# Transposing DMAs of u, q and k on ScalarE's queue, and in all groups of the second MLP's first quarter

## The chip, the cores and the metric

The kernel runs on one core of a Trainium2 chip. A core has a matrix engine (TensorE, PE in the profile), two engines for elementwise work that this kernel uses all the time (VectorE, DVE, and ScalarE, ACT), a third that it hardly uses (GpSimd, POOL), a sequencer without a datapath (SyncE, SP), and 16 DMA engines. Each of the five has its own queue of instructions and runs it in order; they wait for one another by semaphores. A DMA is issued by an instruction in the queue of some engine, which stands in that queue like any other. The metric is the time on the device of one execution, in microseconds (us).

## The reference

Two layers over 256 tokens of 2048 features, in float32. Layer 0 mixes tokens by a convolution module, layer 1 by differential attention; each is followed by an MLP with squared ReLU, and each sub-layer has a scale, a shift and a gate made from a condition vector `c`:

```
mod = silu(c) @ ada_w[i] + ada_b[i]            # six vectors of 2048 per layer
h = x * (1 + scale) + shift
x = LayerNorm(alpha * x + gate * f(h))
f = conv module | differential attention       # layer 0 | layer 1
f = square(relu(h @ w1 + b1)) @ w2 + b2        # MLP: 2048 -> 8192 -> 2048
attention: q, k, v = split(h @ w_qkv); rope on q and k; 16 heads of 128 in 8 pairs;
           a = softmax(q1 k1) - lam * softmax(q2 k2); o = rmsnorm(a v) @ w_o
```

## The kernel before

The 256 tokens are two tiles, t = 0 and 1, of 128 partitions. A matmul takes the activations with features on the partitions as its stationary operand (called `h`, `u` or `attno` in their turned form) and weights 512 columns wide as its moving one, so an output has tokens on the partitions and has to be turned before it can feed the next product. To keep float32's accuracy each operand is held as a high and a low part, and a product is three matmuls: high by high (L702), high by low part of the weight (L704), low by high (L705).

**The weights.** They arrive by DMA from SP, 1 MB at a time (L638), which is two tiles of 128 rows and 512 columns for each of two halves. Each half is cast by ACT to its high part (L657, `wh_...`), VectorE subtracts for the low part (L659, `wl_...`), and PE then runs 12 matmuls on it. A group (512 output columns, all 2048 inputs) is 8 such halves. Loads and casts run four halves ahead of PE (`AHEAD = 4`). Rows of the condition matrices that are needed later come between them as loads of 1 MB too (L421), and VectorE makes dot products of them (L230).

**MLP 1** has four quarters q of its 8192 hidden features. A quarter is four groups g of w1 (512 hidden features each) and then four groups of w2. When a w1 group ends, its output for t = 0 and t = 1 has to be biased, squared, turned and split into `u_hi` (ACT, L515) and `u_lo` (VectorE, L518). There are two ways. By PE: ACT copies the output (L1483, `us`), PE transposes four blocks of 128 (L1488, `ut`), VectorE adds, rectifies and squares (L1501, L1504). By DMA: ACT copies the float32 bits into two planes of 16-bit halves (L1417, `uh`), a transposing DMA turns them (L1419, `ux`, 128 x 8 x 128), ACT puts the halves together again (L1423, `r`), and VectorE works on that (L1431, L1432). `by_dma(i, q, g)` chooses. Work that follows later is put off by `defer(n, fn)`, n halves of weights: 2 halves for PE's way (`U_WAIT`), 4 for the DMA's in layer 1 (`T_WAIT`).

**Attention** has groups of q, k and v in turn, four heads of each at a time (g = 0 to 3). `rope_evac` rotates q and k on VectorE (L1657 to L1665), ACT splits the result into two planes (L1669), a transposing DMA turns them (L1674, `qkx_q`, `qkx_k`), and four halves later ACT joins them (L1680, `qT`, `kT`). Only k's last group is turned by PE (L1686, L1689). The softmaxes (`at_sm`, L1719), the norms (`at_on`, L1750, L1753) and the turned outputs (`attno_hi`, L515; `attno_lo`, L518) of the group before lie between these on ACT and VectorE.

The order of PE's and VectorE's instructions follows the program and its deferrals. The order on ACT and SP is set by a scheduler that builds a timeline of the whole kernel; an instruction that comes to ACT therefore also changes what it puts where around it.

Of the kernel before, what the change touches and what calls it, by code (L numbers as in the profile page):

```python
# [82 lines left out]
def group_order(s):  # L83

    return list(range(NGRP))[::1 if (len(SLICES) - s) % 2 else -1]
# [72 lines left out]
def trunk(  # L158
# [8 lines left out]
    nc = tc.nc  # L167
# [16 lines left out]
    def tp_tile(name):  # L184
        return ps_tp[0].tile([P, 512], F32, tag="tp", name=name)
# [57 lines left out]
    def defer(n, fn):  # L243
        put_off.append((ticks[0] + n, fn))
# [265 lines left out]
    def put_split(pair, c0, n, s0, ns, src, eng=None, trail=False):  # L510

        hi, lo = pair
        h = hi[:, c0:c0 + n, s0:s0 + ns]
        l = lo[:, c0:c0 + n, s0:s0 + ns]
        nc.scalar.copy(h, src)  # L515

        def low():
            (eng or nc.vector).tensor_tensor(l, src, h.bitcast(F32), op=ALU.subtract)  # L518
        if trail:
            trailing.append(low)  # L520
        else:
            low()
# [739 lines left out]
    for s, (f0, nf) in enumerate(SLICES):  # L1262
# [6 lines left out]
        for pos, k in units:  # L1269
            g = group_order(s)[pos]  # L1270
# [3 lines left out]
            if (s, h) in X_AT:  # L1274
                a, b = X_AT[s, h]
# [8 lines left out]
            if nf > 1 or pos % 2 == 0:  # L1284
                parts = w_parts.pop(0)
# [14 lines left out]
            if not last and h >= END_AT[s]:  # L1300
                n = h - END_AT[s] - 1 + (s + 1 < BOTH_PE)
# [106 lines left out]
        defer(4 + q, lambda q=q: alpha_x(q))  # L1408

    def by_dma(i, q, g):  # L1410
        return i == 1 and (q > 0 or g == 3)

    def halves_t(t, ps, uT, i, q, g, n0):

        name = f"{i}_{q}_{g}_{t}"
        parts = work.tile([P, 2, NG], U16, tag="X", name=f"uh_{name}", bufs=3)
        nc.scalar.copy(parts, ps.bitcast(U16).rearrange("p (n b) -> p b n", b=2))  # L1417
        turned = work.tile([P, 2, 4, P], U16, tag="A", name=f"ux_{name}")
        nc.sync.dma_start_transpose(turned.rearrange("p b a n -> p (b a) n"), parts.rearrange("p b n -> p (b n)"))  # L1419

        def rest():
            r = work.tile([P, 4, P], F32, tag="B", name=f"r_{name}")
            nc.scalar.copy(r.rearrange("p a n -> p (a n)").bitcast(U16).rearrange("p (a n b) -> p a n b", a=4, b=2),  # L1423
                           turned.rearrange("p b a n -> p a n b"))
            f0 = i * 64 + n0 // P
            if i == 0:
                for j in range(4):
                    nc.scalar.activation(r[:, j, :], r[:, j, :], AF.Relu, bias=cv["b1c"][:, f0 + j:f0 + j + 1])
                nc.vector.tensor_tensor(r, r, r, op=ALU.mult)
            else:  # L1430
                nc.vector.tensor_tensor(r, r, cv["b1c"][:, f0:f0 + 4].unsqueeze(2).broadcast_to([P, 4, P]), op=ALU.add)  # L1431
                nc.vector.scalar_tensor_tensor(r, r, 0.0, r, ALU.max, ALU.mult)  # L1432
            put_split(uT, g * 4, 4, t * P, P, r, trail=True)
        defer(T_WAIT[i], rest)
# [218 lines left out]
    def rope_evac(nm, g, kv):  # L1653
        def on_t(t, ps):
            ph = ps.rearrange("p (h d) -> p h d", h=4)
            p1 = work.tile([P, 4, P], F32, tag="A", name=f"rp1_{nm}{g}{t}")
            nc.vector.tensor_tensor(p1.rearrange("p h (b d) -> p (h b) d", b=2),  # L1657
                                    ps.rearrange("p (h d) -> p h d", d=64),
                                    at["cos"][:, t, :].unsqueeze(1).broadcast_to([P, 8, 64]), op=ALU.mult)
            p2 = work.tile([P, 4, P], F32, tag="B", name=f"rp2_{nm}{g}{t}")  # L1660
            nc.vector.tensor_tensor(p2[:, :, 0:64], ph[:, :, 64:128],
                                    at["sinN"][:, t, :].unsqueeze(1).broadcast_to([P, 4, 64]), op=ALU.mult)
            nc.vector.tensor_tensor(p2[:, :, 64:128], ph[:, :, 0:64],
                                    at["sinP"][:, t, :].unsqueeze(1).broadcast_to([P, 4, 64]), op=ALU.mult)
            nc.vector.tensor_tensor(p1, p1, p2, op=ALU.add)  # L1665

            if (nm, g) != ("k", 3):
                parts = p2.rearrange("p h n -> p (h n)").bitcast(U16).rearrange("p (b n) -> p b n", b=2)
                nc.scalar.copy(parts, p1.rearrange("p h n -> p (h n)").bitcast(U16).rearrange("p (n b) -> p b n", b=2))  # L1669
                if t == 0:  # L1670
                    turned = late["pool"].tile([P, 2, 4, P], U16, tag="qkx", name=f"qkx_{nm}{g}{t}")
                else:
                    turned = work.tile([P, 2, 4, P], U16, tag="A", name=f"qkx_{nm}{g}{t}")
                nc.sync.dma_start_transpose(turned.rearrange("p b a n -> p (b a) n"),  # L1674
                                            parts.rearrange("p b n -> p (b n)"))

            def joined():
                if t == 0:
                    kv[nm] = work.tile([P, 4, S], F32, tag="X", name=f"{nm}T_{g}", bufs=3)
                nc.scalar.copy(kv[nm].bitcast(U16).rearrange("p h (n b) -> p h n b", b=2)[:, :, t * P:(t + 1) * P, :],  # L1680
                               turned.rearrange("p b h n -> p h n b"))

            def rest():
                pt = tp_tile(f"qkt_{nm}{g}{t}")
                for h in range(4):
                    nc.tensor.transpose(out=pt[:, h * P:(h + 1) * P], in_=p1[:, h, :], identity=ident)  # L1686
                if t == 0:
                    kv[nm] = work.tile([P, 4, S], F32, tag="X", name=f"{nm}T_{g}", bufs=3)
                nc.scalar.copy(kv[nm][:, :, t * P:(t + 1) * P], pt.rearrange("p (h n) -> p h n", h=4))  # L1689
            if (nm, g) != ("k", 3):  # L1690
                defer(4, joined)
            else:
                defer(3, rest)
        return on_t
# [233 lines left out]
```

## Time and profile before

| | us |
|---|---|
| median of 3 runs | 2267.64 (2267.3 to 2270.41) |
| the profiled execution | 2264.22 |
| its span, first to last instruction | 2262.3 |
| PE busy | 2223.8 (98%) |
| VectorE busy | 1713.5 (76%) |
| ScalarE busy | 1139.8 (50%) |

The granted clock of TensorE is 0.996 over the span. All DMAs of the kernel are issued by SP: loads of 1 MB for weights and condition rows, and 40 transposing ones of 256 KB: 8 for q, 6 for k and 26 for the `u` of MLP 1. In the rows of the profile an engine's name with q behind it (SPq, ACTq) is its queue, where issuing is shown; `x2` stands for two instructions drawn together; what stands in brackets is the idle time of the engine before an instruction and whose end finished it. PE's rows overlap, since matmuls are pipelined.

### The profile page before, as it was taken

What the parts mean: (1) busy time and instruction counts of PE and PEld (TensorE: products, weight loads), DVE (VectorE), ACT (ScalarE), POOL (GpSimd) and SP (SyncE); (2) the same over time, 40 slices, a digit from 0 to 9 for tenths busy, and PEclk for the clock granted to TensorE, in tenths of its full rate; (3) what the DMA queues carried; (4) which work ended last, traced back from release to release, by engine and by line L of the source; (5) the groups of instructions that cost most, each with busy time, mean ns of one, the idle gap of its engine ahead of it and who ended that gap; (6) DMA issues with size and microseconds to landing.
All of it is one profiled execution on the core that took longest, in us unless ns stands there. A gap on an engine that the chain in (4) does not pass through costs nothing.

```text
span 2262.3 us, 28005 instructions
## 1 busy us (share of the span) xinstructions
PE 2223.8 (98%) x10900; PEld 1779.6 (79%) x10900; DVE 1713.5 (76%) x2124; ACT 1139.8 (50%) x1528; POOL 38.2 (2%) x53
## 2 busy tenths in 40 slices
PE   8999999999999999999999999999999999999999
PEld 5677657687888888888878788787888888888886
DVE  7688889778977888878878877887965665665567
ACT  4336773564355355355365555545444643643652
POOL 0000000000000000000000010100000000000000
PEclk9999999999999999999999999999999999999999
DMA  9996789699988888888858876875976765766773
GB/s 397 419 392 270 298 323 397 218 340 330 349 301 315 308 290 319 320 306 287 292 168 280 270 228 213 288 272 178 331 247 199 209 211 191 224 202 192 220 239 111
DMA packets 259712, 619.04 MB, mean 274 GB/s; under 512 B 52623, under 2 KB 52851, under 8 KB 230011
## 3 DMA queue, kind: packets, MB, share of 16 engines
q1 hardware_dynamic: 259580, 617.27, 77.9%
q8 instruction: 85, 1.39, 0.3%
q14 instruction: 47, 0.38, 0.0%
HBM read 604.59 MB, written 2.15 MB: 268 GB/s over the span
## 4 chain that ended last, share of the span: by engine, by line
PE 85%; DVE 7%; DMA 3%; ACT 3%; issue 1%; POOL 0%; SPq 0%; ACTq 0%; DVEq 0%; POOLq 0%
PE w_ps L704 20%; PE w_ps L705 20%; PE w_ps L702 19%; PE pw_ps L600 2%; PE pw_ps L601 2%; PE pw_ps L602 2%; PE cv L936 1%; PE pw_ps L702 1%; PE pw_ps L705 1%; PE pw_ps L704 1%; PE qkv_q_ps L705 1%; PE qkv_q_ps L702 1%; PE qkv_v_ps L704 1%; PE qkv_q_ps L704 1%; PE qkv_v_ps L705 1%
## 5 line engine op out<-in xcount | busy, mean ns | idle before, releaser
L657 ACT CAST wh_w<-w_w 128x1024 fp32r<-128x1024 f32 x512 | 535.9, 1053 | 658.1 <-PE w_ps L705 507.9
L659 DVE TENSOR_TENSOR wl_w<-w_w,wh_w 128x1024 fp32r<-128x1024 f32 x510 | 613.6, 1222 | 314.5 <-ACT wh_w L657 314.1
L702 PE MATMUL w_ps<-wh_w,hm_hi 128*128 128x512 f32 x1024 | 401.0, 392 | 2.5 <-ACT hm_hi L515 2.5
L705 PE MATMUL w_ps<-wh_w,hm_lo 128*128 128x512 f32 x1024 | 399.6, 390 | 1.6 <-DVE hm_lo L518 1.6
L704 PE MATMUL w_ps<-wl_w,u_hi 128*128 128x512 f32 x1024 | 399.1, 390 | 1.6 <-DVE wl_w L659 1.6
L702 PE MATMUL w_ps<-wh_w,u_hi 128*128 128x512 f32 x1024 | 399.1, 390 | 0.0
L704 PE MATMUL w_ps<-wl_w,hm_hi 128*128 128x512 f32 x1024 | 399.0, 390 | 0.0
L705 PE MATMUL w_ps<-wh_w,u_lo 128*128 128x512 f32 x1024 | 398.5, 389 | 0.0
L230 DVE SCALAR_TENSOR_TENSOR adaw<-adaw,cond_rows 128x2048 f32<-128x2048 f32 x108 | 246.8, 2285 | 0.2 <-DMA adaw<-in_ada_rows_dram 0.2
L702 PEld LDWEIGHTS w_ps<-wh_w,hm_hi 128*128 128x128 f32 x1024 | 192.7, 188 | 44.1 <-ACT hm_hi L515 4.1
L704 PEld LDWEIGHTS w_ps<-wl_w,u_hi 128*128 128x128 f32 x1024 | 192.3, 188 | 43.4 <-DVE wl_w L659 3.8
L705 PEld LDWEIGHTS w_ps<-wh_w,hm_lo 128*128 128x128 f32 x1024 | 192.6, 188 | 42.9 <-DVE hm_lo L518 2.9
L702 PEld LDWEIGHTS w_ps<-wh_w,u_hi 128*128 128x128 f32 x1024 | 192.3, 188 | 40.2
L704 PEld LDWEIGHTS w_ps<-wl_w,hm_hi 128*128 128x128 f32 x1024 | 192.6, 188 | 39.5
L705 PEld LDWEIGHTS w_ps<-wh_w,u_lo 128*128 128x128 f32 x1024 | 192.3, 188 | 39.8
L600 PE MATMUL pw_ps<-wh_pw,h_hi 128*128 128x512 f32 x256 | 103.9, 406 | 2.6 <-ACT wh_pw L582 1.9
L601 PE MATMUL pw_ps<-wl_pw,h_hi 128*128 128x512 f32 x256 | 100.8, 394 | 0.9 <-DVE wl_pw L585 0.8
L602 PE MATMUL pw_ps<-wh_pw,h_lo 128*128 128x512 f32 x256 | 100.5, 393 | 0.0
L585 DVE TENSOR_TENSOR wl_pw<-w_pw,wh_pw 128x1024 fp32r<-128x1024 f32 x64 | 77.3, 1221 | 28.9 <-ACT wh_pw L582 28.7
L582 ACT CAST wh_pw<-w_pw 128x1024 fp32r<-128x1024 f32 x64 | 65.9, 1051 | 44.8 <-PE pw_ps L602 25.3
L600 PEld LDWEIGHTS pw_ps<-wh_pw,h_hi 128*128 128x128 f32 x256 | 48.4, 189 | 29.6 <-issue 13.0
L518 DVE TENSOR_TENSOR u_lo<-r,u_hi 128x512 fp32r<-128x512 f32 x64 | 43.5, 689 | 28.4 <-ACT u_hi L515 28.2
(355 smaller groups left out, 3012.1 us busy)
## 6 DMA issues: line engine op xcount, KB each, us to landing
w_w<-in_mlp_w_dram SPq DMA_DIRECT2D x256, 1024.0 KB, 5.9
adaw<-in_ada_rows_dram SPq DMA_DIRECT2D x108, 1024.0 KB, 6.7
w_pw<-in_pw_tiles_dram SPq DMA_DIRECT2D x32, 1024.0 KB, 12.4
ad<-in_ada_rows_dram SPq DMA_DIRECT2D x25, 1024.0 KB, 8.5
w_pw<-in_conv_pw_w_dram SPq DMA_DIRECT2D x16, 1024.0 KB, 9.1
w_qkv_q<-in_attn_qkv_w_dram SPq DMA_DIRECT2D x16, 1024.0 KB, 5.4
w_qkv_k<-in_attn_qkv_w_dram SPq DMA_DIRECT2D x16, 1024.0 KB, 5.1
w_qkv_v<-in_attn_qkv_w_dram SPq DMA_DIRECT2D x16, 1024.0 KB, 7.1
```

Of the source, the lines that this page charges most:

```text
L230: nc.vector.scalar_tensor_tensor(w, w, 1.0, cond_rows, ALU.mult, ALU.mult, accum_out=m[:, ch:ch + 1])
L518: (eng or nc.vector).tensor_tensor(l, src, h.bitcast(F32), op=ALU.subtract)
L582: nc.scalar.copy(hq, rq)
L585: nc.vector.tensor_tensor(lq, rq, hq.bitcast(F32), op=ALU.subtract)
L600: nc.tensor.matmul(pss[t], lhsT=xh, rhs=wh, start=(kc == first), stop=False)
L601: nc.tensor.matmul(pss[t], lhsT=xh, rhs=wl, start=False, stop=False)
L602: nc.tensor.matmul(pss[t], lhsT=xl, rhs=wh, start=False, stop=(kc == last))
L657: nc.scalar.copy(hi, rq)
L659: eng.tensor_tensor(lo, rq, hi.bitcast(F32), op=ALU.subtract)
L702: nc.tensor.matmul(pss[tt], lhsT=xh, rhs=wh, start=(kc == 0 and job["bias"] is None), stop=False)
L704: nc.tensor.matmul(pss[tt], lhsT=xh, rhs=wl, start=False, stop=False)
L705: nc.tensor.matmul(pss[tt], lhsT=xl, rhs=wh, start=False, stop=(kc == nk - 1))
```

## The change

All transposing DMAs are issued on ScalarE's queue, where SP issued them before. And `by_dma` now says yes for every group of layer 1, so that groups 0 to 2 of quarter 0 are turned by DMA as well.

```diff
     def by_dma(i, q, g):
-        return i == 1 and (q > 0 or g == 3)
+        return i == 1
...
         parts = work.tile([P, 2, NG], U16, tag="X", name=f"uh_{name}", bufs=3)
         nc.scalar.copy(parts, ps.bitcast(U16).rearrange("p (n b) -> p b n", b=2))
         turned = work.tile([P, 2, 4, P], U16, tag="A", name=f"ux_{name}")
-        nc.sync.dma_start_transpose(turned.rearrange("p b a n -> p (b a) n"), parts.rearrange("p b n -> p (b n)"))
+        nc.scalar.dma_start_transpose(turned.rearrange("p b a n -> p (b a) n"), parts.rearrange("p b n -> p (b n)"))
...
                     turned = work.tile([P, 2, 4, P], U16, tag="A", name=f"qkx_{nm}{g}{t}")
-                nc.sync.dma_start_transpose(turned.rearrange("p b a n -> p (b a) n"),
-                                            parts.rearrange("p b n -> p (b n)"))
+                nc.scalar.dma_start_transpose(turned.rearrange("p b a n -> p (b a) n"),
+                                              parts.rearrange("p b n -> p (b n)"))
```

So 46 transposing DMAs stand in ACT's queue (40 moved, 6 new); 24 PE transposes and 6 copies `us` are gone, and 6 copies `uh` and 6 copies `r` have come. SP's other instructions keep their order. Three places show how the instructions now stand.

On ACT at q's group 1 (the two copies L1669 of t = 0 and t = 1, the joined copies `qT`, casts of k's weights, and work of the attention of group 0), before:

```order
L1669 COPY rp_q_10093<-rp_q_10091 128x1024
L657 CAST wh_qkv_k_2_0_10150<-w_qkv_k_2_10148 128x1024
L1669 COPY rp_q_10102<-rp_q_10100 128x1024
L1680 COPY qT_10207<-qkx_q_10098 128x4x256
L657 CAST wh_qkv_k_2_1_10180<-w_qkv_k_2_10148 128x1024
L1680 COPY qT_10207<-qkx_q_10107 128x4x256
L1719 ACTIVATE at_1_1_sm,at_1_1_zs<-at_1_1_sm,at_1_1_mx 128x256 x2
L1750 ACTIVATE at_1_0_on,at_1_0_ss<-at_1_0_o 128x256
L657 CAST wh_qkv_k_3_0_10214<-w_qkv_k_3_10212 128x1024
L515 CAST attno_hi<-at_0_1_o_10167 128x2x128
```

and now:

```order
L1669 COPY rp_q_10093<-rp_q_10091 128x1024
L657 CAST wh_qkv_k_2_0_10150<-w_qkv_k_2_10148 128x1024
L1674 DMA_TRANSPOSE qkx_q_10098<-rp_q_10093 128x8x128
L1669 COPY rp_q_10102<-rp_q_10100 128x1024
L1680 COPY qT_10207<-qkx_q_10098 128x4x256
L1674 DMA_TRANSPOSE qkx_q_10107<-rp_q_10102 128x8x128
L657 CAST wh_qkv_k_2_1_10180<-w_qkv_k_2_10148 128x1024
L1719 ACTIVATE at_1_1_sm,at_1_1_zs<-at_1_1_sm,at_1_1_mx 128x256 x2
L1750 ACTIVATE at_1_0_on,at_1_0_ss<-at_1_0_o 128x256
L657 CAST wh_qkv_k_3_0_10214<-w_qkv_k_3_10212 128x1024
L1680 COPY qT_10207<-qkx_q_10107 128x4x256
L515 CAST attno_hi<-at_0_1_o_10167 128x2x128
```

The second transfer now stands behind the copy that waits for the first to land, and the second joined copy has moved down to just ahead of `attno_hi`.

On ACT behind the first w1 group of quarter 1 of MLP 1, before:

```order
L1417 COPY uh_1_0_0_14055<-w_1_1_0_ps_13917 128x1024
L1417 COPY uh_1_0_1_14059<-w_1_1_0_ps_13918 128x1024
L657 CAST wh_w_1_1_1_1_1_14065<-w_w_1_1_1_1_14037 128x1024
L657 CAST wh_w_1_1_1_2_0_14083<-w_w_1_1_1_2_14081 128x1024
L1423 COPY r_1_0_0_14115<-ux_1_0_0_14057 128x1024
L1423 COPY r_1_0_1_14120<-ux_1_0_1_14061 128x1024
L657 CAST wh_w_1_1_1_2_1_14099<-w_w_1_1_1_2_14081 128x1024
```

and now:

```order
L1417 COPY uh_1_0_0_14043<-w_1_1_0_ps_13905 128x1024
L1417 COPY uh_1_0_1_14047<-w_1_1_0_ps_13906 128x1024
L657 CAST wh_w_1_1_1_1_1_14053<-w_w_1_1_1_1_14025 128x1024
L1419 DMA_TRANSPOSE ux_1_0_0_14045<-uh_1_0_0_14043 128x8x128
L1419 DMA_TRANSPOSE ux_1_0_1_14049<-uh_1_0_1_14047 128x8x128
L657 CAST wh_w_1_1_1_2_0_14071<-w_w_1_1_1_2_14069 128x1024
L1423 COPY r_1_0_0_14103<-ux_1_0_0_14045 128x1024
L1423 COPY r_1_0_1_14108<-ux_1_0_1_14049 128x1024
L657 CAST wh_w_1_1_1_2_1_14087<-w_w_1_1_1_2_14069 128x1024
```

Both transfers stand together between two casts, with one cast between them and the copies `uh` that they read.

On VectorE behind group 1 of quarter 0, which was turned by PE (L230 and L842 are work of the condition vectors and of the norm), before:

```order
L230 SCALAR_TENSOR_TENSOR adaw_5_11_12940,mod_5_11778<-adaw_5_11_12940,cond_rows 128x2048
L1501 TENSOR_TENSOR r_0_1_0_12962<-ut_0_1_0_12957,vec_101 128x512
L1504 SCALAR_TENSOR_TENSOR r_0_1_0_12962<-r_0_1_0_12962 128x512
L1501 TENSOR_TENSOR r_0_1_1_12971<-ut_0_1_1_12966,vec_101 128x512
L1504 SCALAR_TENSOR_TENSOR r_0_1_1_12971<-r_0_1_1_12971 128x512
L518 TENSOR_TENSOR u_0_lo<-r_0_1_0_12962,u_0_hi 128x4x128
L518 TENSOR_TENSOR u_0_lo<-r_0_1_1_12971,u_0_hi 128x4x128
L659 TENSOR_TENSOR wl_w_1_0_2_2_0_12980<-w_w_1_0_2_2_12977,wh_w_1_0_2_2_0_12979 128x1024
L659 TENSOR_TENSOR wl_w_1_0_2_2_1_12996<-w_w_1_0_2_2_12977,wh_w_1_0_2_2_1_12995 128x1024
L230 SCALAR_TENSOR_TENSOR adaw_5_12_12999,mod_5_11778<-adaw_5_12_12999,cond_rows 128x2048
```

and now:

```order
L230 SCALAR_TENSOR_TENSOR adaw_5_11_12940,mod_5_11778<-adaw_5_11_12940,cond_rows 128x2048
L659 TENSOR_TENSOR wl_w_1_0_2_2_0_12960<-w_w_1_0_2_2_12957,wh_w_1_0_2_2_0_12959 128x1024
L659 TENSOR_TENSOR wl_w_1_0_2_2_1_12976<-w_w_1_0_2_2_12957,wh_w_1_0_2_2_1_12975 128x1024
L230 SCALAR_TENSOR_TENSOR adaw_5_12_12979,mod_5_11778<-adaw_5_12_12979,cond_rows 128x2048
L1431 TENSOR_TENSOR r_0_1_0_12994<-r_0_1_0_12994,vec_101 128x512
L1432 SCALAR_TENSOR_TENSOR r_0_1_0_12994<-r_0_1_0_12994 128x512
L1431 TENSOR_TENSOR r_0_1_1_12999<-r_0_1_1_12999,vec_101 128x512
L1432 SCALAR_TENSOR_TENSOR r_0_1_1_12999<-r_0_1_1_12999 128x512
L842 TENSOR_TENSOR z<-z,basem_gb_12955 128x512
L518 TENSOR_TENSOR u_0_lo<-r_0_1_0_12994,u_0_hi 128x4x128
L518 TENSOR_TENSOR u_0_lo<-r_0_1_1_12999,u_0_hi 128x4x128
```

The four operations on `r` come two low parts and one dot product later than before; their number and size are the same.

## The prediction

> **What bounds the kernel now.** I read the page first, to see which engine sets the span, then PE's waits, because only these can be shortened, and then the timelines at the places that the change touches.
>
> ```profile
> span 2262.3 us, 28005 instructions
> PE 2223.8 (98%) x10900; PEld 1779.6 (79%) x10900; DVE 1713.5 (76%) x2124; ACT 1139.8 (50%) x1528; POOL 38.2 (2%) x53
> PE 85%; DVE 7%; DMA 3%; ACT 3%; issue 1%; POOL 0%; SPq 0%; ACTq 0%; DVEq 0%; POOLq 0%
> ```
>
> PE is busy for 98% of the span and makes 85% of the chain of waits. SP's issuing has 0% of that chain. So a shorter queue on SP is worth nothing by itself; the change can gain only where PE has less to do or waits less, and loses where a wait that is now hidden reaches PE. These are PE's waits that lie behind a transposing DMA or just after one, and the one on the last group of MLP 1:
>
> ```profile
> PE qkt_k L1686 <- DVE rp_k L1665: 1.6, 2, 1.3
> PE w_ps L704 <- DVE wl_w L659: 1.6, 4, 0.6
> PE wo_ps L704 <- DVE wl_wo L659: 1.2, 1, 1.2
> PE qkv_k_ps L704 <- DVE wl_qkv_k L659: 1.1, 1, 1.1
> PE qkv_v_ps L704 <- DVE wl_qkv_v L659: 0.9, 1, 0.9
> ```
>
> The columns are the total in us, how many, and the longest. They sum to 6.4 us, 0.28% of the span. No measured difference under 0.2%, about 4.5 us, can be told from no change for this kernel; so the whole gain in sight is near that bound.
>
> **The transposes taken from PE.** Three w1 groups of quarter 0 give up eight PE transposes each.
>
> ```profile
> 1575.97 0.87 PE ut L1488 x8
> ...
> 1621.28 0.87 PE ut L1488 x8
> ```
>
> These are the first and the last of three alike in the chain of waits: 3 x 0.87 = -2.6 us. That is the certain part of PE's work, but it is time only where the engines that feed PE can run faster too. The windows that hold these groups say otherwise (columns: window, length, busy us and count of PE, PEld, DVE, ACT, POOL, granted clock, DMA share, GB/s):
>
> ```profile
> 1575.60:1598.30 22.70, 22.70 (x106) 18.90 (x105) 19.83 (x21) 10.53 (x12) 0.00 (x0) 1.00 0.83 281
> 1598.30:1620.90 22.60, 22.60 (x106) 18.80 (x105) 22.14 (x25) 10.44 (x12) 0.00 (x0) 1.00 0.96 340
> 1620.90:1643.50 22.60, 22.60 (x105) 18.84 (x104) 19.43 (x24) 11.28 (x12) 0.00 (x0) 1.00 0.96 353
> ```
>
> In the same stretch, 1598 to 1645, ACT's waits for loads (total, how many, longest):
>
> ```profile
> ACT wh_w L657 <- DMA w_w<-in_mlp_w_dram: 10.6, 4, 3.3
> ```
>
> A group without its transposes would last 22.6 - 0.87 = 21.7 us. The middle window has 22.14 us of VectorE work, and in the last two the DMA engines are busy for 0.96 x 22.6 = 21.7 us. ACT already waits four times for a load, 10.6 us in all. Into this stretch the change puts two more transposing DMAs per group. What one costs is in the rows of the tile that receives them:
>
> ```profile
> L1419 SPq DMA_TRANSPOSE ux<-uh x26: 1238/1276/4808, 1641.6 to 2166.5; - x26
> DMA to landing us min/median/max: 3.1/3.3/4.1
> ```
>
> Issue takes 1.28 us at the median and landing 3.3 us from the issue's start, so the engines move data for at most 3.3 - 1.28 = 2.0 us per transfer; the lower bound is zero, for a transfer that fits into gaps. In the two windows with a share of 0.96 there are no gaps to speak of, so the loads behind get late by up to 2 x 2 x 2.0 = 8 us; in the first, 0.17 x 22.7 = 3.9 us are free, which is just the 4.0 us that its two need. What takes up lateness is the lead of the weights' low parts over PE:
>
> ```profile
> 1610.17 1.22 DVE L659 TENSOR_TENSOR wl_w<-w_w,wh_w 128x1024 fp32r<-128x1024 f32 x1
> 1613.18 0.39 PE L704 MATMUL w_ps<-wl_w,hm_hi 128*128 128x512 f32 x1
> ```
>
> The part is done at 1611.39 and used at 1613.18: 1.8 us of lead. Half of the upper bound, 4 us, less one lead of 1.8 us is 2.2 us; and the 0.87 us that VectorE refuses in the middle window (22.14 against 21.7) is 0.4 more. I take +3 us, bounds 0 and 8 us: the stretch gives its own gain back.
>
> **The queue of ACT in attention.** Eight of q's transfers and six of k's now stand in ACT's order. Around q's group 1 the trace has:
>
> ```profile
> 1248.99 3.55 SPq L1674 DMA_TRANSPOSE qkx_q<-rp_q  x2
> 1252.59 0.75 SPq L638 DMA_DIRECT2D w_qkv_k<-in_attn_qkv_w_dram  x1
> 1253.77 1.17 ACT L1680 COPY qT<-qkx_q 128x1024 uint16<-128x1024 uint16 x1 [2.49 <-DMA qkx_q<-rp_q]
> 1255.79 1.16 ACT L1680 COPY qT<-qkx_q 128x1024 uint16<-128x1024 uint16 x1
> 1259.32 0.40 ACT L515 CAST attno_hi<-at_o 128x256 fp32r<-128x256 f32 x1
> 1260.70 1.22 DVE L659 TENSOR_TENSOR wl_qkv_k<-w_qkv_k,wh_qkv_k 128x1024 fp32r<-128x1024 f32 x1
> 1266.65 0.50 PE L704 MATMUL qkv_k_ps<-wl_qkv_k,ha_hi 128*128 128x512 f32 x1 [1.11 <-DVE wl_qkv_k L659]
> ```
>
> SP's two issues, 3.55 us with the wait for the second copy, end before it sends the next weight load at 1252.59. In the new order of ACT the first transfer is issued inside the 2.49 us that ACT now idles, so it costs nothing. The second stands behind the joined copy that waits for the first to land: its issue of 1.24 us falls on busy ACT, the second joined copy drops behind two exponentials, a norm and a cast, and the cast attno_hi behind that. Without new idle time attno_hi starts one issue later, 1260.6 for 1259.32. VectorE's attno_lo and the low weight part follow on its queue, and PE, which already waits 1.11 us there, waits 1.2 to 1.3 more. Queued behind are the remaining casts of k's weights, for which VectorE and then PE wait: +1.3 us.
>
> The same pieces in the same order stand at q's group 3. There VectorE idles for attno_hi as well, and the chain ends at the two waits on rope's last group, 1.6 us together:
>
> ```profile
> 1400.18 1.17 ACT L1680 COPY qT<-qkx_q 128x1024 uint16<-128x1024 uint16 x1 [0.74 <-DMA qkx_q<-rp_q]
> 1402.86 0.51 ACT L1719 ACTIVATE at_sm<-at_sm,at_mx 128x256 f32<-128x256 f32 x1 [0.56 <-DVE at_mx L1716]
> 1404.71 1.05 ACT L657 CAST wh_qkv_k<-w_qkv_k 128x1024 fp32r<-128x1024 f32 x1 [0.75 <-DMA w_qkv_k<-in_attn_qkv_w_dram]
> 1407.52 0.43 DVE L518 TENSOR_TENSOR attno_lo<-at_o,attno_hi 128x256 fp32r<-128x256 f32 x1 [2.00 <-ACT attno_hi L515]
> ```
>
> ACT's idle time in the three rows is 0.74 + 0.56 + 0.75 = 2.05 us, so of two issues, 2.5 us, some 0.5 us is left: +0.5 us. The other groups of q and k have no PE wait of their own in the list above, apart from v's 0.9 us; there I count 0. Together +2 us. Upper bound: three of the listed waits, in k, v and rope, deepened by a full issue each, 3 x 1.28 = +3.8 us. Lower bound: these three vanish because SP, without its 3.55 us, sends its load earlier, -(1.1 + 0.9 + 1.6) = -3.6 us. I stay on the positive side because each wait ends on VectorE behind ACT and none on a load.
>
> **The queue of ACT in the 13 groups of MLP 1 that turn by DMA already.** One group, from its copies to PE's first use of what follows:
>
> ```profile
> 1749.62 1.93 ACT L1417 COPY uh<-w_ps 128x1024 uint16<-128x1024 uint16 x2 [0.99 <-PE w_ps L705]
> 1750.66 2.62 SPq L1419 DMA_TRANSPOSE ux<-uh  x2
> 1751.43 1.06 ACT L657 CAST wh_w<-w_w 128x1024 fp32r<-128x1024 f32 x1
> 1753.02 1.05 ACT L657 CAST wh_w<-w_w 128x1024 fp32r<-128x1024 f32 x1 [0.53 <-PE w_ps L705]
> 1753.98 2.32 ACT L1423 COPY r<-ux 128x1024 uint16<-128x1024 uint16 x2
> 1763.39 1.22 DVE L659 TENSOR_TENSOR wl_w<-w_w,wh_w 128x1024 fp32r<-128x1024 f32 x1
> 1766.65 0.39 PE L704 MATMUL w_ps<-wl_w,hm_hi 128*128 128x512 f32 x1
> ```
>
> After the change both issues stand between the two casts. If ACT's sequencer issues them while its datapath is still in the first cast, they run from 1751.5 to 1754.05, the second cast starts there in place of 1753.02, and the two r copies end at 1757.4 in place of 1756.30: 1.1 us late. If the issue begins only when the cast is over, it is 2.1 us. The lead at the end of the chain is 1766.65 - (1763.39 + 1.22) = 2.04 us. So a group costs 0 by the first reading and 0.1 by the second: 0 to 1.3 us for 13 groups, and I take 0. This is the term with the thinnest cover: everything over 2.04 us goes to PE thirteen times.
>
> In the three groups of quarter 0 the same work is new to ACT. Of the copy that it replaces the trace has this row:
>
> ```profile
> L1483 ACT COPY us<-w_ps x6: 587/587/587, 1572.6 to 1618.6; 128x512 f32<-128x512 f32 x6
> ```
>
> For each transfer that is 2.32 / 2 = 1.16 us of r, 1.28 of issue and 1.93 / 2 - 0.59 = 0.38 of uh, 5.6 us a group, on an engine that the windows show busy for 10 to 11 of 22 us; without that room it would cost those 5.6 us. I count 0.
>
> In the last group of quarter 3 the transfers stand behind the final layer norm's two loads:
>
> ```profile
> 2164.42 6.88 SPq L1419 DMA_TRANSPOSE ux<-uh  x2
> 2164.42 9.43 DMA ux<-uh
> ```
>
> ACT's queue frees them of that, 9.43 us against some 4.6 for two issues and a landing, but of PE's four waits on low parts of the MLPs, 1.6 us in the first fence of waits, none is over 0.6: I take -0.2 us.
>
> **The sum.** -2.6 + 3.0 + 2.0 + 0 - 0.2 = +2.2 us. The profiled execution took 2264.22 us around its span of 2262.3, so it would take 2266.4; the median of the runs is 2267.64, 3.4 us above the profiled one, and the forecast in those terms is 2269.9, so 2270 us, or +0.1%: no change that can be measured. By the terms' bounds together (not all at one end) it lies between 2265 and 2275.
>
> **The rivals.** *First, slower: the transfers are stretched by the loads.* Today transfers and weight loads leave SP one after the other: the load at 1753.78 follows the second transfer's issue.
>
> ```profile
> 1753.78 5.12 SPq L638 DMA_DIRECT2D w_w<-in_mlp_w_dram  x2
> ```
>
> From ACT the second would be issued from 1752.8 to 1754.05, so its 2.0 us of data run beside that load. Were the DMA engines to alternate between two queues, it would land up to 2.2 us later, at 1758.3; the first r copy no longer hides that, and the second starts 2.0 us after its new slot of 1756.3. Its end is then 3.1 us later than now against 2.04 of lead: +1.0 us per group, 13 groups of MLP 1 and 3 of quarter 0 at 0.3 more: 13 + 4, less what the sum already counts in quarter 0, some +12 us, 2282. It decides as soon as the landing of the second transfer exceeds its present 3.3 us by about 1.1. Against it: the longest landing of all 26 today is 4.1, with loads all around. The trace of before has only one queue for all this, so it can't refuse it. The Trainium skill speaks for it: "DMA: Bandwidth & Descriptors", section "Queues, rings and completion order", says that each DMA engine takes turns between the queues that have work, a packet at a time, and its section "Issuing engines are not separate DMA queues" that issuing from several engines saves only the time of the sequencer. By that rule this rival holds; no run here shows it yet.
>
> *Second, faster: SP's block was the cost.* With the loads of attention leaving up to 3.55 us earlier and nothing late on ACT, the five waits listed first shrink to nothing and the transposes' 2.6 us are kept: at most -6.4 - 2.6 = -9, and by half of the waits 2267.6 - 5.8 = 2262. For it speaks the 3.55 us in which SP stands; against it, that SP has 0% of the chain.
>
> *Third, slower: ACT's issues don't overlap and block.* One SP issue took 4.81 us (the largest of the 26). Were an issue on ACT to wait like that in most groups, ACT would be 2.1 + 2 = 4 us late against 2.04: +2 us x 13 = 26, 2296. The median of 1.28 speaks against it.
>
> *Fourth: the moves do nothing, only quarter 0 counts*: -2.6 kept, 2265. That is inside the forecast's range.
>
> **How the numbers follow.** The forecast, with the fourth rival inside it, has 0.47; the first rival 0.30, the second 0.17, the third 0.06. Faster by over 0.2% is the second rival, 0.17. Slower takes the first and third and a little of the forecast's upper edge (2272.2 to 2275): 0.38. The rest, 0.45, is within 0.2%. The likeliest case's own range is 2265 to 2275; to leave out no more than 2 in 10, the range takes the first rival up to 2283 and the faster one down to 2262.
>
> **What would show it right or wrong.** Right: 24 fewer PE transposes, the three windows of quarter 0 no shorter than 22.3 us, the wait of k's low part at 2.3 to 2.5 us, no PE wait in quarters 1 to 3, transfers landing in 3.3 us. Wrong towards slower: a PE wait of about 1 us on u_hi, u_lo or wl_w once in each group of quarters 1 to 3, with landings over 4.4 us. Wrong towards faster: windows of 21.7 us in quarter 0, and attention's waits gone. If PE's sum of waits agrees but the time doesn't, a term I do not have is at work.

## The result: 1.3% slower, and where the time came from

The changed kernel takes 2298.94 us, median of four runs (2294.25 to 2302.49), where the kernel before takes 2268.59 beside it: a ratio of 1.0132, with a 95% interval from 1.0111 to 1.0153. That is 30 us; the forecast was 2270 with a range that ended at 2283.

From the page of the changed kernel, its span, the engines' busy times and its DMA queues (packets, MB, share of 16 engines):

```profile
span 2292.4 us, 27954 instructions
PE 2233.1 (97%) x10876; PEld 1781.5 (78%) x10876; DVE 1713.2 (75%) x2124; ACT 1148.1 (50%) x1534; POOL 40.1 (2%) x53
q1 hardware_dynamic: 217340, 606.78, 74.7%
q10 hardware_dynamic: 48576, 12.06, 3.5%
```

PE does the same matmuls less 24 transposes, and VectorE and ScalarE work as long as before. What is new is a second queue, q10: ScalarE's transfers no longer stand in line with SP's loads in q1. PE's waits of the changed kernel:

```profile
PE w_ps L702 <- ACT wh_w L657: 10.0, 3, 4.8
PE w_ps L704 <- DVE wl_w L659: 9.7, 8, 3.1
PE qkv_k_ps L704 <- DVE wl_qkv_k L659: 5.3, 2, 2.7
```

Before, these were none, 1.6 and 1.1. To see where the time arises I took, in both profiles, the moment at which PE first uses the low part of each of the 672 half tiles of weights; the growth of the difference between two halves is the delay that arises between them. Here it is for the changed kernel and every experiment below, each against the profiled execution of the kernel before (us; attention is its q, k and v groups from their fourth half on, since no transfer is issued ahead of that; quarter 0 runs from the start of its second group to the end of its fourth; the last group is what follows quarter 3's w1 groups). The expectations below have 18.8 for quarter 0, counted behind the first of PE's gains of 0.9 us, and 3.1 for the last group, an earlier reckoning.

| kernel | attention | quarter 0 | rest of MLP 1 | last group |
|---|---|---|---|---|
| changed | 6.7 | 17.9 | 0.0 | 3.6 |
| ScalarE's queue, old groups (e1) | 11.5 | 0.0 | 0.1 | 5.6 |
| SP's queue, all groups (e2) | -0.2 | 7.4 | 0.0 | -0.2 |
| q and k alone on ScalarE's queue (e3) | 8.2 | 0.5 | 0.0 | 0.7 |
| changed, rows in 2 KB pieces (e4) | 14.6 | 12.0 | 6.0 | 8.7 |
| 22 late u transfers on ScalarE's queue (e5) | 0.3 | 0.0 | 0.0 | 0.5 |
| the same, with extra loads (e6) | -0.2 | 0.0 | 30.6 | 0.4 |
| SP's queue, with extra loads (e7) | 0.1 | 0.0 | 0.0 | 0.3 |
| changed, thin rows (e8) | 7.9 | 5.8 | 0.4 | 2.8 |
| e3 with both transfers first (e9) | 8.7 | 0.0 | 0.0 | 0.5 |
| SP's queue, all groups, thin rows (e10) | -0.3 | 4.5 | 0.0 | 0.8 |
| six new transfers alone on ScalarE's queue (e11) | 0.6 | 18.6 | 0.3 | 0.3 |
| 24 late u transfers, final loads later (e12) | -0.3 | 0.0 | 0.0 | -0.5 |

The three places of the changed kernel give 28.2 of the 30.1 us by which its span is longer. The rest arises ahead of the attention and in its first halves, where the program is the same; there, around wo and ahead of quarter 0 other rows have up to 4.3 us as well, from one execution to the next.

The windows of quarter 0 in the changed kernel (length, busy us of PE, PEld, DVE, ACT, POOL with counts, granted clock, DMA share, GB/s):

```profile
1583.90:1605.80 21.90, 21.32 (x94) 17.32 (x93) 19.79 (x20) 12.65 (x15) 0.00 (x0) 1.00 0.90 288
1605.80:1631.60 25.80, 18.32 (x73) 14.42 (x73) 16.35 (x18) 10.02 (x11) 0.00 (x0) 0.83 0.92 258
1631.60:1661.00 29.40, 22.07 (x92) 17.50 (x92) 20.18 (x24) 13.13 (x14) 0.00 (x0) 0.91 1.05 272
```

The group that now begins at 1605.8 shows why. Its timeline, both transfers and who waits for them:

```profile
1604.83 1.35 ACTq L1419 DMA_TRANSPOSE ux<-uh  x1
1606.22 5.57 ACTq L1419 DMA_TRANSPOSE ux<-uh  x1
1607.95 2.59 SPq L638 DMA_DIRECT2D w_w<-in_mlp_w_dram  x2
1611.91 2.00 ACT L657 CAST wh_w<-w_w 128x1024 fp32r<-128x1024 f32 x2 [5.25 <-issue]
1616.05 1.17 ACT L1423 COPY r<-ux 128x1024 uint16<-128x1024 uint16 x1 [2.14 <-DMA ux<-uh]
1622.93 1.16 ACT L1423 COPY r<-ux 128x1024 uint16<-128x1024 uint16 x1 [5.71 <-DMA ux<-uh]
1625.09 0.80 PE L702 MATMUL w_ps<-wh_w,hm_hi 128*128 128x512 f32 x1 [4.34 <-ACT wh_w L657]
1629.02 0.79 PE L704 MATMUL w_ps<-wl_w,hm_hi 128*128 128x512 f32 x1 [3.13 <-DVE wl_w L659]
```

Two things happen to ScalarE, one after the other. It can't finish issuing the second transfer for 5.57 us, and the casts of the weights behind it stand. Then it waits twice for a transfer to land, the second time until 1622.93, 16.7 us after that transfer's issue began; the next cast stands behind that copy, and PE runs dry. The rows of the tile over all its transfers say the same (longest issue 8.57 us, longest landing 13.3 among those that the view could pair):

```profile
L1419 ACTq DMA_TRANSPOSE ux<-uh x32: 1248/1348/8568, 1582.2 to 2192.1; - x32
DMA to landing us min/median/max: 3.0/3.4/13.3
```

Why a transfer takes so long is in the packets. Counted from the trace, packets that began in each microsecond on the 16 engines together, in this group:

```
us from the start     1609  1610  1611  1612  1613  1614  1615  1616  1617  1618  1619
SP, 2 KB                 0     0    18    33    56    77   106   127   160   137   126
SP, 8 KB (rows)         46    29     1     0     0     0     0     0     0     3     3
ScalarE, 256 bytes      36   281   619   113    96    73   107   129   203   187   141
```

From 1614 on the two queues advance by about one packet each in turn, whatever the packets' sizes (73 to 77, 107 to 106, 129 to 127). In the last group of MLP 1 it is the same beside packets of 8 KB: from 2196 to 2200 ScalarE's queue begins 59, 53, 81, 86 and 136 packets in a microsecond, SP's 48, 48, 70, 83 and 133. A transposing DMA has 1024 packets of 256 bytes, 64 per engine, so beside a queue of loads that always has work it needs 64 turns. At 1617 SP begins 160 packets, 10 per engine, so a turn takes some 0.1 us and the 64 some 6.4 us, by estimate. In this group 936 packets of the first transfer had begun by the end of 1611, and the second took from 1613 to 1621. With everything in SP's queue (e2, below) 1843 of the 2048 packets of such a pair begin within three microseconds, with 18 packets of loads among them. The Trainium skill states the rule: "DMA: Bandwidth & Descriptors", section "Queues, rings and completion order", has each DMA engine go round between the queues that have work, a packet at a time. The counts from 1614 and from 2196 agree, with one of the trace's packets to a turn.

Turns are not all of it. From 1612 to 1616 the engines count as busy as from 1616 to 1619 (1.16 and 1.19), and move half as much (164 and 342 GB/s):

```profile
1612.00:1616.00 4.00, 4.00 (x19) 3.34 (x18) 3.01 (x3) 1.91 (x2) 0.00 (x0) 1.00 1.16 164
1616.00:1619.00 3.00, 3.00 (x14) 2.46 (x14) 2.85 (x4) 1.17 (x1) 0.00 (x0) 1.00 1.19 342
```

A load's packet of 2 KB that begins at 1612 takes 0.25 us in the mean; at 1618, and at 1608 ahead of the transfers, it takes 0.084. So single packets can get slower when both queues have work. Why they do is not shown by any run here.

### The profile page after: what moved, and what is told of

It reads as the page before. It is cut to its first block, busy times and chain, and to the rows that moved or that the text cites. A ratio compares the mean times of both kernels' runs of the same rounds, so it can differ in the third digit from the quotient of the medians.

```text
span 2292.4 us, 27954 instructions
## 1 busy us (share of the span) xinstructions
PE 2233.1 (97%) x10876; PEld 1781.5 (78%) x10876; DVE 1713.2 (75%) x2124; ACT 1148.1 (50%) x1534; POOL 40.1 (2%) x53
## 5 line engine op out<-in xcount | busy, mean ns | idle before, releaser
L230 DVE SCALAR_TENSOR_TENSOR adaw<-adaw,cond_rows 128x2048 f32<-128x2048 f32 x108 | 246.8, 2285 | 0.0
```

The source lines that it names most:

```text
L230: nc.vector.scalar_tensor_tensor(w, w, 1.0, cond_rows, ALU.mult, ALU.mult, accum_out=m[:, ch:ch + 1])
```

## The experiments

Theory A, after the comparison of the traces: a transfer on a queue of its own takes turns with the loads in flight and with those that SP now sends earlier, and is late wherever loads stand thick (many of them in flight). The rivals: each transfer on ScalarE's queue costs about the same (B); the six new transfers are the cost on whatever queue (C); the engines share by bytes, or are simply full (D, F); or ScalarE's order is at fault, the prediction's own view.

**e1: the queue alone.** The groups are chosen as before.

```diff
     def by_dma(i, q, g):
-        return i == 1
+        return i == 1 and (q > 0 or g == 3)
```

> The transposing DMAs on ScalarE's queue, the groups of MLP 1 as before (quarter 0's groups 0 to 2 by PE). Theory A (a transfer on a queue of its own takes turns with the loads in flight, packet by packet, so it is late only where loads stand thick: attention and quarter 0 with their condition rows, and the last group with the final norm's rows): the 18.8 us of delay that arose in groups 0 to 2 go, the delay of attention (6.7 us) and of the last group (3.1) stays: 2268.6 + 10, 2276 to 2281. Rival B (every transfer on ScalarE's queue costs about the same): 30 x 40/46 = 26 us, 2295. Rival C (the six new transfers are the cost, the queue is not): 2269.

Measured: 2282.72 us, ratio 1.0071 (1.0054 to 1.0087). The delay of quarter 0 is gone, which refutes B; that of attention and of the last group stays, which refutes C as the whole cause. Attention and the last group cost 17 us here and 10 in the changed kernel, so the time is nearly 2 us above the 2281 that I had expected at most. The same transfers are stretched by different amounts in different kernels.

**e2: the groups alone**, all transfers on SP's queue.

```diff
-        nc.scalar.dma_start_transpose(turned.rearrange("p b a n -> p (b a) n"), ...)
+        nc.sync.dma_start_transpose(turned.rearrange("p b a n -> p (b a) n"), ...)
```

> All groups of MLP 1 by DMA, but all transfers on SP's queue as before. Theory A: in one queue a transfer is served whole before the loads issued after it, so it lands in about 3 to 6 us; the stretch gives back what PE saves: 2266 to 2271. Rival C (quarter 0 has no room for six more transfers, on whatever queue): the 18.8 us of delay stay, 2283 to 2288.

Measured: 2277.19 us, ratio 1.0041 (1.0026 to 1.0056): between the two theories. The six transfers cost 7.4 us in quarter 0 on SP's queue too, net of the transposes that PE no longer does; so of the 17.9 us of the changed kernel 10.5 belong to the queue. I had expected none. SP's queue in that group shows what replaces it:

```profile
1601.75 7.05 SPq L1419 DMA_TRANSPOSE ux<-uh  x2
1608.91 1.07 SPq L638 DMA_DIRECT2D w_w<-in_mlp_w_dram  x2
```

Now SP stands for 7.05 us with the transfers, and the two weight loads leave at 1608.91. In the profile of the kernel before, at the same place, they leave at 1598.76; of the 10.2 us between, 5 are delay from further ahead. Neither queue has a free place for these six transfers: on SP's they hold back the loads, on ScalarE's the loads hold back them.

**e3: q and k alone.** The kernel before with only the 14 transfers of attention on ScalarE's queue.

```diff
-                nc.sync.dma_start_transpose(turned.rearrange("p b a n -> p (b a) n"),
+                nc.scalar.dma_start_transpose(turned.rearrange("p b a n -> p (b a) n"),
```

> Only the 14 transfers of q and k on ScalarE's queue; those of MLP 1 on SP's, groups as before. Theory A: the delay of attention alone, 6.7 us: 2273 to 2277, with first joined copies that wait 2 us longer than before at q's groups 1 and 3. Rival B: 30 x 14/46 = 9 us, 2278. If ScalarE's order alone were at fault (my prediction's view), +2 us, 2270.5.

Measured: 2279.05 us, ratio 1.0049 (1.0031 to 1.0067); 2 us above the range expected, with 8.2 us of delay in attention and the rest outside of what was changed. The first joined copies wait no longer than before (1.91 us for 2.49 at group 1, none for 0.74 at group 3), against the expectation; the second ones do, 2.83 and 5.67 us, where none waited for a transfer before. The 2 us of the prediction's view are refuted. B's 2278 can't be told from this alone, but e1 and e5 exclude it.

**e9: both transfers first.** As e3, and each joined copy stays behind the second transfer in ScalarE's order.

```diff
+                with tc.issue_after(raws["turn"].ins):
-                nc.scalar.copy(kv[nm].bitcast(U16)...
+                    nc.scalar.copy(kv[nm].bitcast(U16)...
```

> As the run with only q's and k's transfers on ScalarE's queue (2279, +12), but each joined copy is kept behind the second transfer in ScalarE's order, so the second is issued without waiting for the first to land. If ScalarE's order is what costs (the second transfer issued 2.7 us late), attention's delay of 8 to 10 us falls by half or more: 2270 to 2274. If the loads that SP now sends ahead are the cost (theory A), the second transfer still lands behind them and most stays: 2275 to 2280.

Measured: 2276.61 us, ratio 1.0039 (1.0026 to 1.0053). Its nine runs lie between 2269.51 and 2282.45, so the time alone speaks only weakly for theory A. In the profiled one attention still loses 8.7 us, but in another place: all of it arises at q's group 1, where e3 lost 2.8, and the 5.4 that e3 lost at group 3 are gone. Around q's group 1 the timeline of this run reads:

```profile
1250.78 0.38 SPq L638 DMA_DIRECT2D w_qkv_k<-in_attn_qkv_w_dram  x1
1251.39 1.26 ACTq L1674 DMA_TRANSPOSE qkx_q<-rp_q  x1
1252.99 0.33 SPq L421 DMA_DIRECT2D adaw<-in_ada_rows_dram  x1
1266.30 1.16 ACT L1681 COPY qT<-qkx_q 128x1024 uint16<-128x1024 uint16 x1 [6.59 <-DMA qkx_q<-rp_q]
1269.41 0.80 PE L704 MATMUL qkv_k_ps<-wl_qkv_k,ha_hi 128*128 128x512 f32 x1 [7.44 <-DVE wl_qkv_k L659]
```

The second transfer is issued at 1251.39, close to where SP issued it before, and is usable at 1266.30, 14.9 us later. In the kernel before, the weight load left after the transfers, at 1252.59; here it leaves at 1250.78, ahead of the second one, and the load of condition rows follows. The order on ScalarE was not what made it late there. At group 3 issuing earlier did help: e3's wait of PE of 4.4 us is gone. But the order of transfer and loads doesn't tell the two groups apart. At group 3 too the weights' load leaves ahead of the second transfer (1407.30 for 1407.62) and the rows' load behind it (1409.51), and there the transfer is usable at 1414.02, 6.4 us after its issue. Nor are the loads thick at group 1. While the second transfer passes, the engines count as busy and move 60 GB/s:

```profile
1257.00:1265.00 8.00, 4.97 (x23) 3.74 (x21) 1.48 (x3) 1.05 (x1) 0.58 (x1) 0.97 1.04 60
```

Some of the rows' packets of 8 KB take over 2.4 us there, 0.31 elsewhere. That the second queue costs attention its delay is shown by e3 and e9 against the kernel before. How much, and at which group, is not explained by turns, and no run here shows what makes the packets slow.

**e11: the six new transfers alone on ScalarE's queue**, all groups by DMA, the other 40 on SP's.

```diff
-        return i == 1 and (q > 0 or g == 3)
+        return i == 1
...
-        nc.sync.dma_start_transpose(turned...
+        (nc.scalar if q == 0 and g < 3 else nc.sync).dma_start_transpose(turned...
```

> All groups of MLP 1 by DMA; only the six new transfers (quarter 0, groups 0 to 2) on ScalarE's queue, the other 40 on SP's. If the parts add up: what six transfers cost on SP's queue (+8 to 10) and what their own queue adds in this stretch (18.8 - 8.3 = 10.5): 2285 to 2289, with no delay in attention or in the last group.

Measured: 2286.10 us, ratio 1.0072 (1.0051 to 1.0093), with 18.6 us in quarter 0 and nothing in attention or in the last group. So the part of quarter 0 stands by itself. The others don't simply add: attention and the last group make 10.3 us in the changed kernel and 17.1 in e1.

**e4, e8 and e10: are the condition rows the thick load?** e4 issues each load of condition rows in four pieces, packets of 2 KB for 8 KB.

```diff
-            nc.sync.dma_start(w, ada_rows[ADA_ROWS[i, v, ch]])
+            for c in range(4): nc.sync.dma_start(w[:, c * 512:(c + 1) * 512], ada_rows[...][:, c * 512:(c + 1) * 512])
```

> The changed kernel with each load of condition rows of layer 1 issued as four pieces of 512 columns, so packets of 2 KB (about 85 ns each) instead of 8 KB (about 310 ns); bytes and order are the same. Theory A with turns by packet: a transfer's 64 packets per engine pass three times faster between packets of 2 KB, its landing in quarter 0 falls from up to 13 us to 5 to 8, and half or more of the 18.8 us of quarter 0 and some of attention's 6.7 go: 2280 to 2290. Rival D (the engines share by bytes, or quarter 0 is just full): no change, 2297 to 2301, or slower for the smaller packets.

Measured: 2310.70 us, ratio 1.0191 (1.0174 to 1.0208), 12 us slower than the changed kernel: the expectation fell. Quarter 0 itself improved (17.9 to 12.0), but attention (6.7 to 14.6), the rest of MLP 1 (0.0 to 6.0) and the last group (3.6 to 8.7) got worse. In the group counted above large packets of rows can't have been the main lever: from 1611 to 1617 all but one of the loads' packets are of 2 KB. What the smaller pieces cost by themselves was not measured.

e8 is the changed kernel, e10 the kernel of e2, both with the eight loads of rows in quarter 0 cut to a quarter:

```diff
+            thin = (i, v) == (1, G_F) and ch >= 8
-            nc.sync.dma_start(w, ada_rows[ADA_ROWS[i, v, ch]])
+            nc.sync.dma_start(w[:, :512] if thin else w, ada_rows[ADA_ROWS[i, v, ch]][:, :512 if thin else D])
...   (the dot product of a thin load runs over its 512 columns four times)
```

> The changed kernel with the eight loads of condition rows in MLP 1's quarter 0 cut to their first 512 columns (6 MB of loads left out; the dot products run over those columns four times, in the same number of elements, so these eight results are not the reference's). Theory A: with thinner loads the transfers land in 3 to 6 us there and most of quarter 0's 18.8 us of delay goes: 2280 to 2287. If the loads' bytes have nothing to do with it and ScalarE's order is at fault: no change, 2297 to 2301.

> All groups of MLP 1 by DMA on SP's queue (2277, +10) with the eight loads of condition rows in quarter 0 cut to their first 512 columns, as in the run with thin rows (6 MB left out, eight results not the reference's). Theory F (the DMA engines are full there, so what the new transfers take comes off the loads): with room the cost goes and PE's 2.6 us stay: 2263 to 2268. If the new transfers cost for ScalarE's added copies instead, no change: 2275 to 2279.

Measured: e8 2287.96 us, ratio 1.0086 (1.0071 to 1.0101), 1 us above the range expected; e10 2272.04 us, ratio 1.0017 (1.0008 to 1.0027). In quarter 0 the thin rows take 12.1 us off ScalarE's queue (17.9 to 5.8) and 2.9 off SP's (7.4 to 4.5). So the bytes of loads in flight decide most of what the second queue costs there: with 6 MB fewer, the difference between the queues is 1.3 us where it was 10.5. e10 was expected at no loss and kept 4.5 us, so full DMA engines are not all of what six transfers cost on SP. In e10's queue of SP the transfers still hold it for 4.93 us and the weight loads leave at 1604.08:

```profile
1599.05 4.93 SPq L1424 DMA_TRANSPOSE ux<-uh  x2
1604.08 1.08 SPq L643 DMA_DIRECT2D w_w<-in_mlp_w_dram  x2
```

I take the rest to be that hold; neither it nor ScalarE's added copies, the other rival, was tested apart.

**e5, e6 and e7: the same in a quiet place.** In quarters 1 to 3 the changed kernel lost nothing. e5 moves only those transfers, without the last group's.

```diff
-        nc.sync.dma_start_transpose(turned...
+        (nc.scalar if q > 0 and (q, g) != (3, 3) else nc.sync).dma_start_transpose(turned...
```

> Only the 22 transfers of MLP 1's quarters 1 to 3 without the last group are on ScalarE's queue; all others on SP's, groups as before. Theory A (late only where loads stand thick): in these quarters the loads leave gaps, so 0, within 3 us of the kernel before, transfers landing in 3.4 us and no wait of PE. Rival B (every transfer on ScalarE's queue costs): 30 x 22/46 = 14 us, 2281.

e6 is e5, and e7 the kernel before, with a load of 1 MB behind each of these groups' copies (the last line makes it wait for the copy uh of t = 1); nobody reads what it brings:

```diff
+        if t == 1 and q > 0 and (q, g) != (3, 3):
+            extra = cond_rows.rearrange("p (a n) -> p a n", a=4)
+            more = nc.sync.dma_start(extra, mlp_w1[1].rearrange("(kc p) n -> p kc n", p=P)[:, 0:4, 0:NG])
+            tc.add_manual_dep(more.ins, copied.ins.name, ...)
```

> The kernel of the run before (22 transfers on ScalarE's queue) with one more load of 1 MB, 512 packets of 2 KB, which nobody reads, issued by SP behind each of these 11 groups' copies. Theory A: the two transfers of a group take turns with it and the next weights, land in 6 us or more in place of 3.4, ScalarE's second issue takes longer, and PE waits 1 to 4 us in each of 11 groups: 10 to 40 us over the run before. Rival D (the engines have room, turns don't matter): the same as the next run's surplus, 0 to 5 us.

> The same 11 loads of 1 MB, but all transfers on SP's queue as in the kernel before, the load right behind the two transfers. Theory A: one queue serves the transfers first, so they land in 3.3 us as before and only the weights behind get 2.9 us later, which their lead takes up: 0 to 5 us over the kernel before, far less than the run before.

Measured: e5 2266.19 us, ratio 0.9997 (0.9988 to 1.0006); e6 2295.12 us, ratio 1.0102 (1.0061 to 1.0143), its four runs between 2276 and 2297; e7 2267.22 us, ratio 0.9998 (0.9988 to 1.0007). The same 11 MB cost 30.6 us of delay in these quarters with ScalarE's queue and nothing with SP's. One group of e6:

```profile
1797.17 1.25 ACTq L1419 DMA_TRANSPOSE ux<-uh  x1
1798.08 0.37 SPq L1423 DMA_DIRECT2D cond_rows<-in_mlp_w_dram  x1
1798.52 3.48 ACTq L1419 DMA_TRANSPOSE ux<-uh  x1
1802.11 1.05 ACT L657 CAST wh_w<-w_w 128x1024 fp32r<-128x1024 f32 x1 [3.10 <-issue]
1813.73 1.16 ACT L1429 COPY r<-ux 128x1024 uint16<-128x1024 uint16 x1 [5.70 <-DMA ux<-uh]
```

and the same group of e7:

```profile
1773.45 2.61 SPq L1419 DMA_TRANSPOSE ux<-uh  x2
1776.11 0.58 SPq L1423 DMA_DIRECT2D cond_rows<-in_mlp_w_dram  x1
1776.77 2.39 ACT L1429 COPY r<-ux 128x1024 uint16<-128x1024 uint16 x2
```

In e7 both transfers are in the queue before the extra load and the r copies start 3.3 us after the first issue. In e6 the extra load slips in between the two issues; the second issue takes 3.48 us and its transfer is usable 15.2 us after it began. Between e6 and e7 the queue of the transfers is all that was changed, and the place of the extra load follows from it. Both of the changed kernel's symptoms, the long issue and the late landing, come with the second queue where a load is in flight.

**e12: the last group.** All 24 late transfers on ScalarE's queue, and the final norm's loads 8 halves later.

```diff
-        nc.sync.dma_start_transpose(turned...
+        (nc.scalar if q > 0 else nc.sync).dma_start_transpose(turned...
...
-                last["begin"]()
+                defer(8, last["begin"])
```

> All 24 transfers of MLP 1's quarters 1 to 3, the last group's two among them, on ScalarE's queue; the final norm's two loads of 1 MB are issued 8 halves later, so they don't stand beside the last group's transfers. Theory A: no delay in the last group (the changed kernel had 3 us there), within 2 us of the kernel before: 2265 to 2269. If the last group's delay came from ScalarE's queue itself: 3 us stay.

Measured: 2266.56 us, ratio 0.9996 (0.9987 to 1.0006), -0.5 us in the last group. In the changed kernel this group has the same picture as quarter 0:

```profile
2190.33 0.42 SPq L1807 DMA_DIRECT2D fin<-in_ln_ffn_b_dram  x1
2192.10 8.57 ACTq L1419 DMA_TRANSPOSE ux<-uh  x1
2200.79 2.95 ACT L657 CAST wh_w<-w_w 128x1024 fp32r<-128x1024 f32 x3 [8.43 <-PE w_ps L704]
2210.46 0.50 PE L704 MATMUL w_ps<-wl_w,u_hi 128*128 128x512 f32 x1 [1.54 <-DVE wl_w L659]
```

The second issue takes 8.57 us beside the final loads, and ScalarE's casts resume at 2200.79, just when it is over (the view names another releaser, which had long been done). With those loads out of the way the delay is gone.

No version here beats the kernel before; e5 and e12 equal it.

## Why the prediction was wrong

**PE's transposes, -2.6 us: right, and worth nothing in the end**, as the prediction said of this term. In the changed kernel PE's delay shrinks by 0.9 us at each of the three places. Behind the first it stays away, and that window is 21.90 us long where the prediction wanted at least 22.3; behind the other two the delay grows by more.

**Quarter 0, +3 us, at most 8: wrong, 17.9 net of the 2.6 saved, 20.5 gross.** Two steps failed. The data time of at most 2.0 us per transfer was taken from transfers that had a queue to themselves once their turn came; in the group shown above the two were usable 9.9 and 11.1 us after their issues had ended. And "the loads behind get late" was the only price; the transfers themselves getting late, and ScalarE standing in its issue, were not in the sum. Without the second queue the term would still have been mis-sized: 7.4 net plus 2.6 is 10.0 gross on SP's queue, over the bound of 8.

**Attention, +2 us, at most 3.8: wrong, 6.7, and 8.2 to 11.5 in e3 and e1.** The prediction counted the issues in ScalarE's order and let each transfer land after 3.1 us as on SP. It read the 3.55 us in which SP stood as harmless to lose. At q's group 1 that standing kept the next loads behind the transfers (1252.59 before, 1250.78 in e9); that this was the protection is an inference from the traces, and group 3 of e9 doesn't need it.

**The 13 groups that DMA turned already, 0: right** for twelve of them, all but the last group, with the lead unchanged. In quarter 1's first group, in the changed kernel:

```profile
1776.05 1.93 ACT L1417 COPY uh<-w_ps 128x1024 uint16<-128x1024 uint16 x2 [0.98 <-PE w_ps L705]
1777.09 1.26 ACTq L1419 DMA_TRANSPOSE ux<-uh  x1
1777.86 1.06 ACT L657 CAST wh_w<-w_w 128x1024 fp32r<-128x1024 f32 x1
1778.39 1.36 ACTq L1419 DMA_TRANSPOSE ux<-uh  x1
1780.83 2.25 ACT L1423 COPY r<-ux 128x1024 uint16<-128x1024 uint16 x2
1789.82 3.49 DVE L659 TENSOR_TENSOR wl_w<-w_w,wh_w 128x1024 fp32r<-128x1024 f32 x3
1793.07 0.39 PE L704 MATMUL w_ps<-wl_w,hm_hi 128*128 128x512 f32 x1
```

The low part that PE uses at 1793.07 is done at 1789.82 + 1.22 = 1791.04: 2.03 us of lead, as before the change. The 1.1 us that I had ScalarE lose did not reach it: the first transfer is issued while the second copy uh still runs, the second beside the cast.

**The last group, -0.2 us: wrong, +3.6.** The prediction saw that the transfers would leave the line behind the final loads and counted this as a gain. They left it to take turns with them, as the counts from 2196 show.

**The sum.** In the prediction's terms the profile shows -2.6 + 20.5 + 6.7 + 0 + 3.6 = 28.2 us in place of +2.2. (In the prediction's own sum 2266.4 and 3.4 make 2269.8, not 2269.9; nothing hangs on it.)

**The first rival had much of the mechanism and the wrong place.** It let the engines alternate between two queues, priced the second transfer of the 13 groups at +1.0 us, quarter 0 at 0.3 more, and put the end at 2282. What it needs are loads in flight, and it was priced where the loads leave gaps. Against it stood that no landing exceeded 4.1 us "with loads all around"; with one queue for all, that row can't speak about two. **The third rival**, ScalarE blocked by an issue, came true in quarter 0, at 5.57 us in the group shown, and in the last group, at 8.57, though not in "most groups". Most of the chance of slower, 0.38, was put on these two. Both show in the result, but neither forecast its places or its size.

## What to carry to other kernels

Here small transposing transfers that stood in one queue with large loads were served nearly whole and held back the loads behind them. On a second queue they took turns, packet by packet, with what the first queue had in flight, some packets became slower besides, and the first queue sent its loads sooner. So before moving a latency-critical DMA off a busy queue, count its packets and look what is in flight at that moment: with gaps it was free, beside loads a wait of 3.3 us for a transfer became one of 6 to 17 here. Plain transfers without a transpose were not tried. And a queue that seems to be blocked by such transfers may be what keeps the loads out of their way.

## What the runs showed of the hardware that I had not expected

An engine that issues a DMA into a queue with its previous transfer still unfinished can stand in the issue: 5.57, 4.14 and 8.57 us in the changed kernel, for issues of 1.25 us otherwise. On ScalarE the casts behind such an issue stood too (5.25 us in the group shown). Where nothing was in the way, the issues of 1.26 and 1.36 us at 1777.09 and 1778.39 ran beside a copy and a cast.

A long wait cost PE more than the wait. In quarter 0 of the changed kernel PE waited for 9.1 + 6.2 = 15.3 us, and the delay was 17.9 net of 2.6 saved, 20.5; in the windows the granted clock fell to 0.83 and 0.91, and the matmuls behind the waits took 0.63 us in place of 0.39. The Trainium skill, "TensorE: Matmul & The Clock Gate", section "What's actually happening", has the clock drop after an idle window of about 3.4 us; the two waits of 4.34 and 4.79 us agree with that. In attention a wait of 2.71 us, shorter than the window, was followed by a granted clock of 0.50 from 1267.8 to 1271.1, so shorter waits can cost clock too.

Three things stay open: what the pieces of 2 KB cost by themselves in e4, why the same transfers of attention lost 6.7 us in one kernel and 11.5 in another, and why single packets of both queues take several times as long in some of these encounters.
